# Hybrid trunk layer: decay tables computed among the projection pairs, and neighbourhood attention's first loads moved ahead of the fill's third weight block

## The chip, the cores and the metric

The kernel runs on one core of one Trainium2 chip. Its time is the device time of one execution in microseconds (us); of the kernel before there are three timed runs and one execution recorded by the profiler. Lower is better.

## What is computed

One layer of a hybrid encoder trunk on 1024 tokens of width 1024, in float32. Between two feed-forward blocks stands a token mixer, and only it is touched:

```python
u = rms_norm(x)
rq, rk, rv, rg, nq, nk, nv, g_ret, g_na = split(u @ w_in)
# retention: 4 heads, chunks of 128, forward and backward
lg    = log_sigmoid(decay_logit)                    # one number per head and direction
intra = where(lower, exp(lg * diff), 0)             # 128 x 128 per head
k_dec, q_dec = exp(lg * (127 - i)), exp(lg * (i + 1))
chunk_dec    = exp(lg * 128)
y = retention(rotary(rq), rotary(rk), rv, intra, k_dec, q_dec, chunk_dec)
y_ret = (silu(rg) * headnorm(y)) @ w_ret_out
# neighbourhood attention: 8 heads of 64, a 16 x 64 grid of tokens
y_na  = (softmax(nq nk^T / 8 + bias) nv) @ w_na_out
x = x + rms_norm((sigmoid(g_ret) * y_ret + sigmoid(g_na) * y_na) @ w_out)
```

The "decay tables" are intra for both directions, k_dec, q_dec and chunk_dec: 536 numbers in each of 128 partitions.

## The kernel before, in words

Every float32 operand of a matrix product is split into a high and a low half (`Core.split`, L62 on ScalarE makes the high half, L63 on VectorE the low one; the attention's queries use the scaled form, L65 and L66), and each product is three matmuls, high x high (L89), high x low and low x high (L90, L91). A matmul of 512 columns is the unit of PE's work.

The order of the stages around the change is this.

1. The **pairs** (`Pairs.run`, called in the loop over `jobs` in `trunk_layer`): the projections nq, nk, rq, rk, rg and the first gates, two 128-row weight tiles at a time, by Winograd's scheme with seven products, over the operands a11, s2, a12, s3, s1, a22, s4, in this order at the end of the last pair. Their results pass through `ev` tiles of the pool `pa` and are stored to DRAM by POOL's queue (L69). The weights come through `Core.raw`: a 512 KB block into one of four `wraw` buffers, loaded by SP's queue (L73), cut into two pieces of 512 columns that are split into eight `wh` and eight `wl` buffers.
2. **Neighbourhood attention** (`na_cores`): 4 pairs of heads times 8 units. The first keys (`kraw`, L891) and queries (`qraw`, four loads, L879) are loaded and split; then each unit computes scores (L921 on PE, into two PSUM banks), adds the bias while evacuating them (L922, VectorE), subtracts the maximum and exponentiates (L924, L926), divides (L928, L930), transposes the probabilities (L940, PE), splits them (`pth`, `ptl`) and multiplies them with the values (`vh`, `vl`). Its pool `na` lies in memory that the pairs used.
3. Meanwhile the **fill** gives PE work between the units: a generator, `products()`, whose steps are called by `fill(n)`. Its first products are retention's values, `vproj(wrv[j], ...)`: for three 128-token groups at a time it goes over eight 128-row slices of the weights, two slices to a W block, one step for each group and slice. `fill(n0)` issues 12 steps before the first unit, `fill(n1)` and `fill(n2)` two each in every unit. The first four slices multiply a11, the next four a12.
4. **Retention** (`ret_cores`) then reads the decay tables, which the class `Decays` computes. In the kernel before that happens at unit 12 of the attention, through the dictionary `side`; three small loads on SP (L999, L1018, L1020), some 50 small instructions on VectorE and ScalarE.

Each engine works off its own queue in order. Who stands where in it is decided when the program is built: a scheduler takes the instructions by the order of the code and by when their inputs can be there, so that loads and small instructions may be pulled far ahead of the place where the code has them. Tiles of a new pool wait for the last reader of the memory that they lie in; where a tile lies follows from the order in which the tiles are made. `add_manual_dep` with a `NoSync` dependency makes the scheduler put one instruction behind another and adds no wait.

Of the kernel before, what the change touches and what calls it, by code (L numbers as in the profile page):

```python
# [11 lines left out]
F32 = mybir.dt.float32  # L12
F32R = mybir.dt.float32r
# [6 lines left out]
P = 128  # L20
D = 1024
S = 1024
# [5 lines left out]
RH = 4  # L28
NHP = 4

NA_FILL = (12, 2, 2)
# [8 lines left out]
class Core:  # L40
# [29 lines left out]

    def raw(self, src, n=D):
        raw = self.wpool.tile([P, D], F32, tag="wraw", name="wraw", bufs=4)
        self.nc.sync.dma_start(raw[:, :n], src)  # L73
        return raw

    def piece(self, src, eng=None):

# [494 lines left out]
class LeftFactors:  # L572


    order = [j + h * FT // 2 for j in range(FT // 2) for h in range(2)]
# [289 lines left out]
    return lhs  # L865


def na_cores(c, pool, d, bias, fill, n0, n1, n2, side={}):


    nc = c.nc
    kop, qraw, qop, vop, ots, bts = {}, {}, {}, {}, {}, {}

    def qload(hp):

        qraw[hp] = [pool.tile([P, S], F32, tag="qraw", name="qraw", bufs=2) for _ in range(2)]
        for e in range(2):
            for half in range(2):
                nc.sync.dma_start(qraw[hp][e][64 * half:64 * half + 64], d["nq"][hp][64 * e:64 * e + 64])  # L879

    def qsplit(hp, cb):

# [5 lines left out]

    def load(hp):
        kr = pool.tile([P, S], F32, tag="kraw", name="kraw", bufs=1)  # L890
        nc.sync.dma_start(kr, d["nk"][hp])  # L891

        kop[hp] = [pool.tile([P, S], F32R, tag=f"k{e}", name=f"k{e}", bufs=2) for e in range(2)]
        for e in range(2):
            es, es_ = slice(64 * e, 64 * e + 64), slice(64 - 64 * e, 128 - 64 * e)
            for b in range(2):
                bs = slice(b * 512, b * 512 + 512)
                c.split(kop[hp][e][es, bs], kop[hp][e][es_, bs], kr[es, bs], eng=nc.gpsimd if hp and b else None)
# [60 lines left out]
    units = [(hp, *u) for hp in range(NHP) for u in NA_UNITS]  # L959
    n = len(units)  # L960
    s, pt = {}, {}
    load(0)
    qload(0)
    qsplit(0, 0)
    fill(n0)
    for i in range(n + 2):
        if i < n:
            s[i] = scores(*units[i])
            hp, j = units[i][0], i % 8
            if j == 4 and hp + 1 < NHP:  # L970
                load(hp + 1)
            if j in (0, 1, 4):
                qsplit(hp, {0: 1, 1: 2, 4: 3}[j])
            if j == 5 and hp + 1 < NHP:
                qload(hp + 1)
            if j == 7 and hp + 1 < NHP:
                qsplit(hp + 1, 0)
        if i in side:
            side[i]()
        fill(n1)  # L980
        if 1 <= i <= n:
            hp, _, _, cb = units[i - 1]
            if (hp, cb) not in vop:
                vload(hp, cb)
            pt[i - 1] = flip(s.pop(i - 1))
        if i >= 2:
            hp, _, rg, cb = units[i - 2]
            values(hp, rg, cb, pt.pop(i - 2))
            if (i - 2) % 8 == 7:
                c.store(d["no"][hp], ots[hp].rearrange("p r c -> p (r c)"))  # L990
        fill(n2)


class Decays:
    def __init__(self, c, pool, logits, tabs):
        nc = c.nc
        t = pool.tile([P, 8, 6], F32, name="dect")
        x = pool.tile([P, 8], F32, name="decx")
        nc.sync.dma_start(x, logits)  # L999
        a, e, z, w, s, lg = (t[:, :, i] for i in range(6))  # L1000

        nc.vector.tensor_scalar(a, x, -1.0, None, ALU.mult)
        nc.vector.tensor_tensor(a, a, x, ALU.min)
        nc.scalar.activation(e, a, AF.Exp)
# [11 lines left out]
        self.lg = lg  # L1016
# [4 lines left out]
        self.qd = pool.tile([P, 2, RH], F32, name="decq")  # L1021
        self.kd = pool.tile([P, 2, RH], F32, name="deck")
        self.gc = pool.tile([P, 2, RH], F32, name="decg")
        self.dm = pool.tile([P, RH, P], F32, name="decm")
        for b in range(2):
            ls = lg[:, 4 * b:4 * b + 4]
            nc.vector.tensor_scalar(self.qd[:, b], ls, tb[:, b:b + 1], None, ALU.mult)
            nc.vector.tensor_scalar(self.kd[:, b], ls, tb[:, 2 + b:3 + b], None, ALU.mult)
            nc.vector.tensor_scalar(self.gc[:, b], ls, 128.0, None, ALU.mult)
        for h in range(RH):  # L1030
            nc.vector.tensor_scalar(self.dm[:, h], df[:, 0], lg[:, h:h + 1], None, ALU.mult)
            nc.vector.scalar_tensor_tensor(self.dm[:, h], df[:, 1], lg[:, 4 + h:5 + h], self.dm[:, h],
                                           op0=ALU.mult, op1=ALU.add)
        for q in (self.qd, self.kd, self.gc, self.dm):
            nc.scalar.activation(q, q, AF.Exp)
        for q in (self.kd, self.dm):
            nc.vector.tensor_scalar(q, q, RET_SCALE, None, ALU.mult)
# [172 lines left out]
def trunk_layer(ctx: ExitStack, tc, x, xt, g1a, w1i, w1o, g1b, gma, wmt, wnv, wrv, logits, dtab, rope, bias,  # L1210
                wro, wno, wmo, gmb, g2a, w2i, w2o, g2b, out):
    nc = tc.nc
# [5 lines left out]
    c = Core(tc, const, wpool, psum, dram)  # L1218
    c.small = const
    pad = edge.tile([P, 32], F32, name="edge")  # L1220

    def dt(name, shape):
        return dram.tile(shape, F32, name=name)
# [8 lines left out]
        "sr": dt("sr", [8, P, S]), "sn": dt("sn", [8, P, S]), "z": dt("z", [8, P, S]), "m": dt("m", [8, 2, P, S]),  # L1232
    }

    def rows(a):
# [51 lines left out]
    def xh(t, k):  # L1287

        return a21 if (t, k) == (1, 0) else wx.op(("a11", "a12", None, "a22")[2 * t + k])

    def vproj(src, groups, done):

        for toks in groups:
            banks = {t: c.bank() for t in toks}
            for k in range(KT):
                if k % 2 == 0:
                    w = ahead.pop(k // 2) if k // 2 in ahead else c.load_w(src[k // 2])
                for t in toks:
                    tt = slice((t % 4) * P, (t % 4 + 1) * P)
                    c.mm3(banks[t], [q[:, k % 4, tt] for q in xh(t // 4, k // 4)], w[k % 2], k == 0, k == KT - 1)  # L1300
                    yield
            for t in toks:
                done(t, banks[t])
# [40 lines left out]
    with tc.tile_pool(name="pa", bufs=1, reuse_waits="tile") as pa:  # L1344
# [7 lines left out]
        tabs = [[pa.tile([P, 512], F32, tag="tab", name="tab", bufs=4) for _ in range(2)] for _ in range(2)]  # L1352
# [4 lines left out]
        for i, (_, _, f, g, fn) in enumerate(jobs):  # L1357
# [18 lines left out]
            if i == 2:  # L1376
                x1pool = pool(x1_stack, "x1b", "right")
                a21[:] = [x1pool.tile([P, 4, 512], F32R, name=f"a21{q}") for q in "hl"]
                for k in range(2):
                    raw = c.raw(d["a21"][:, 2 * k:2 * k + 2].rearrange("p k t -> p (k t)"))  # L1380
                    c.split(*[q[:, 2 * k:2 * k + 2].rearrange("p k t -> p (k t)") for q in a21], raw)
            if i == NHP - 1:
                for _ in vproj(wnv, ((4, 5, 6, 7),), done_nv):
                    pass
                for cb in range(4):
                    nc.sync.dma_start(d["nvg"][cb].rearrange("t (r c) d -> (t r) c d", r=4),
                                      d["nv"][:, KEY_OFF[cb]:KEY_OFF[cb] + 32, :])
# [1 line left out]

    m_stack, o_stack = ExitStack(), ExitStack()  # L1390
    mix = pool(m_stack, "mix")
    mix.tile([P, 40], F32, name="pad")
    evpool[:] = [mix]

    def gate(i, dst, halves=(0, 1)):
# [44 lines left out]
            c.store(d["z"][i], e)  # L1440

    fill = Filler(products())
    dec = []
    with tc.tile_pool(name="na", bufs=1, reuse_waits="tile") as na:
        na_cores(c, na, d, bias, fill, *NA_FILL, {12: lambda: dec.append(Decays(c, mix, logits, dtab))})
    dec = dec[0]
    fill.until("rv")
    with tc.tile_pool(name="ret", bufs=1, reuse_waits="tile") as ret:
        ret_cores(c, ret, mix, d, dec, fill, RET_FILL)
# [176 lines left out]
```

## Time and profile before

| | |
|---|---|
| timed runs (3) | 2257.23, 2260.53, 2262.26 us; median 2260.53 |
| profiled execution | 2262.09 us, of which the profile's span is 2260.2 us |
| PE (TensorE matmul) busy | 2200.6 us, 97% |
| DVE (VectorE) busy | 1638.3 us, 72% |
| ACT (ScalarE) busy | 984.0 us, 44% |
| POOL (GpSimd) busy | 581.0 us, 26% |
| mean granted clock of TensorE | 0.992 |

The profile is that of one execution. Its times are microseconds from the start of the span. A timeline row has start, length, engine, line, operation, what it writes and reads, shape and count, and in brackets how long the engine sat idle before it and what ended that. SPq and POOLq are the engines' DMA queues: a row there is the issue of a transfer, not its landing. PEld is TensorE's weight load. The granted clock is the share of full speed that TensorE was given.

The stretch that matters lies near 1000 us: the last pair's last product (s4) ends at 1004, the fill's first matmuls (ps<-wh,a11h) follow, and the first score matmul (L921) starts at 1018.22.

### The profile page before, as it was taken

Reading aid. Unit: us, or ns where it says so; the run is one execution under the profiler, and the core shown is the slowest. Engines: PE = TensorE matmul, PEld = TensorE weight load, DVE = VectorE, ACT = ScalarE, POOL = GpSimd, SP = SyncE. Lnnn points to the kernel's source line nnn. Section 1 sums busy time; section 2 is a strip of 40 time slices with the busy share of each in tenths; the row PEclk is TensorE's granted clock in tenths of the full one; section 3 lists DMA queues with packets and bytes.
Section 4 is the critical chain, followed back from the end, with each engine's and each line's share of the span. In section 5 each row is a group of like instructions: output and inputs, shape, how many; then the busy total and the mean of one; then the engine's idle time right before and its main releaser. Section 6 shows DMA issues by size and latency. Waiting matters only on the chain.

```text
span 2260.2 us, 30006 instructions
## 1 busy us (share of the span) xinstructions
PE 2200.6 (97%) x10200; PEld 1827.2 (81%) x10200; DVE 1638.3 (72%) x2911; ACT 984.0 (44%) x2039; POOL 581.0 (26%) x755
## 2 busy tenths in 40 slices
PE   7899999999998999999999999999999999999998
PEld 5688888888786887878888888888887888888886
DVE  7898878765458757769885678553899887876444
ACT  5444434332334322248885665422544343433232
POOL 1121212158521122311101222111112121215942
PEclk9999999999999999999999999999999999999999
DMA  6354434497545455557655466686445443449864
GB/s 251 131 183 153 177 131 174 176 388 295 201 173 181 168 173 144 146 170 246 218 184 173 151 219 228 250 307 228 145 144 213 146 171 137 154 161 363 297 223 180
DMA packets 155240, 449.34 MB, mean 199 GB/s; under 512 B 19600, under 2 KB 50448, under 8 KB 152976
## 3 DMA queue, kind: packets, MB, share of 16 engines
q1 hardware_dynamic: 112656, 311.09, 39.9%
q0 software_dynamic: 42432, 136.35, 16.6%
q8 instruction: 81, 1.33, 0.2%
q14 instruction: 71, 0.58, 0.1%
HBM read 302.66 MB, written 148.90 MB: 200 GB/s over the span
## 4 chain that ended last, share of the span: by engine, by line
PE 84%; DVE 6%; issue 3%; ACT 3%; DMA 2%; POOL 2%; SPq 0%; POOLq 0%; DVEq 0%; ACTq 0%
PE ps L91 26%; PE ps L90 26%; PE ps L89 26%; PE pt L90 1%; PE pt L91 1%; PE pt L89 1%; POOL rstd L99 1%; DVE wl L63 1%; PE ps L921 1%; PE pt L940 1%; DMA wraw<-in_dram 1%; PE pt L128 0%; POOL ry L69 0%; ACT wh L62 0%; DVE s L922 0%
## 5 line engine op out<-in xcount | busy, mean ns | idle before, releaser
L63 DVE TENSOR_TENSOR wl<-wraw,wh 128x512 fp32r<-128x512 f32 x472 | 316.9, 688 | 63.1 <-ACT wh L62 62.7
L62 ACT CAST wh<-wraw 128x512 fp32r<-128x512 f32 x476 | 274.6, 618 | 175.1 <-PE ps L90 64.3
L89 PE MATMUL ps<-wh,g 128*128 128x512 f32 x548 | 214.1, 391 | 0.4 <-DVE tmp L226 0.4
L90 PE MATMUL ps<-wl,g 128*128 128x512 f32 x548 | 213.5, 390 | 0.0
L91 PE MATMUL ps<-wh,g 128*128 128x512 f32 x548 | 213.3, 389 | 0.0
L562 ACT ACTIVATE c<-c 128x512 f32<-128x512 f32 x88 | 55.4, 632 | 198.0 <-DVE c L527 103.9
L63 DVE TENSOR_TENSOR wl<-w,wh 128x512 fp32r<-128x512 f32 x77 | 76.0, 1005 | 88.3 <-ACT wh L62 88.1
L63 DVE TENSOR_TENSOR wl<-x,wh 128x512 fp32r<-128x512 f32 x77 | 79.2, 1044 | 76.2 <-ACT wh L62 74.8
L89 PEld LDWEIGHTS ps<-wh,g 128*128 128x128 f32 x548 | 102.9, 188 | 21.8 <-DVE tmp L226 0.7
L90 PEld LDWEIGHTS ps<-wl,g 128*128 128x128 f32 x548 | 102.9, 188 | 21.4 <-DVE wl L63 0.5
L91 PEld LDWEIGHTS ps<-wh,g 128*128 128x128 f32 x548 | 102.9, 188 | 21.2
L89 PE MATMUL ps<-a11h,wh 128*128 128x512 f32 x276 | 111.5, 404 | 8.4 <-ACT wh L62 8.4
L62 ACT CAST wh<-t 128x512 fp32r<-128x512 f32 x58 | 36.0, 621 | 190.0 <-DVE t L521 189.9
L91 PE MATMUL ps<-a11h,wl 128*128 128x512 f32 x276 | 109.8, 398 | 6.3 <-DVE wl L63 6.1
L90 PE MATMUL ps<-a11l,wh 128*128 128x512 f32 x276 | 109.7, 398 | 0.1
L91 PE MATMUL ps<-a22h,wl 128*128 128x512 f32 x280 | 109.2, 390 | 0.6 <-DVE wl L63 0.6
L89 PE MATMUL ps<-a22h,wh 128*128 128x512 f32 x280 | 109.7, 392 | 0.0
L89 PE MATMUL ps<-a12h,wh 128*128 128x512 f32 x276 | 108.9, 395 | 0.5 <-ACT ev L1312 0.3
L90 PE MATMUL ps<-a22l,wh 128*128 128x512 f32 x280 | 109.1, 390 | 0.0
L91 PE MATMUL ps<-a12h,wl 128*128 128x512 f32 x276 | 107.7, 390 | 0.0
L90 PE MATMUL ps<-a12l,wh 128*128 128x512 f32 x276 | 107.5, 390 | 0.0
L89 PE MATMUL ps<-s2h,wh 128*128 128x512 f32 x232 | 92.1, 397 | 7.0 <-ACT wh L62 7.0
(430 smaller groups left out, 6290.0 us busy)
## 6 DMA issues: line engine op xcount, KB each, us to landing
wraw<-in_dram SPq DMA_DIRECT2D x204, 512.0 KB, 4.4
g<-g0s SPq DMA_DIRECT2D x44, 512.0 KB, 4.1
g<-g1s SPq DMA_DIRECT2D x44, 512.0 KB, 4.9
g<-g0a SPq DMA_DIRECT2D x33, 512.0 KB, 3.3
g<-g1a SPq DMA_DIRECT2D x33, 512.0 KB, 4.3
g0s<-gth POOLq DMA_DIRECT2D x44, 256.0 KB, 4.7
g0s<-cmb POOLq DMA_DIRECT2D x44, 256.0 KB, 3.7
g1s<-gth POOLq DMA_DIRECT2D x44, 256.0 KB, 4.5
```

The costliest lines, as they stand in the source:

```text
L62: self.done = [nc.scalar.copy(h, src).ins, (eng or nc.vector).tensor_tensor(l, src, hf, ALU.subtract).ins]
L63: (eng or nc.vector).tensor_tensor(l, src, hf, ALU.subtract).ins]
L89: mm(ps, a[0], b[0], start=start, stop=False)
L90: mm(ps, a[0], b[1], start=False, stop=False)
L91: mm(ps, a[1], b[0], start=False, stop=stop)
L99: self.nc.gpsimd.tensor_tensor(r[:, :n], ms, self.mhalf[:, :n], ALU.pow)
L562: nc.scalar.activation(gate[j], gate[j], AF.Silu)
L921: nc.tensor.matmul(bv, q[:, rg * P:(rg + 1) * P], k, start=n == 0, stop=n == 1)
L940: nc.tensor.transpose(pt[:, j * P:(j + 1) * P], s[:, i % 2, (i // 2) * P:(i // 2 + 1) * P], c.ident)
```

## The change

It has two parts.

**The decay tables** are computed in the loop over the jobs of the pairs, after job 3 in the code, into one tile `dec` of the pool `pa`, and stored to a DRAM tensor of the same shape. `Decays.make` is the old computation; the object now only gives views into a 536-wide tile. After `na_cores` the tile is loaded into the pool `mix`, and retention reads it there. With this the `side` dictionary goes, and the tables' tiles and scratch leave `mix`; a pad tile there grows from 40 to 104 columns, which shifts where the later tiles of that side lie.

**The first loads of the attention**: queries are now loaded ahead of the keys; the first output tile `ots[0]` is made between the two key tiles, which moves the second one in memory; and the names of the first loads are collected in `qk`. When the fill loads the W block of its fifth slice (`k > 3`, its third block), `Core.after` puts that load behind them.

```diff
     def raw(self, src, n=D):
         raw = self.wpool.tile([P, D], F32, tag="wraw", name="wraw", bufs=4)
-        self.nc.sync.dma_start(raw[:, :n], src)
+        self.fetch = self.nc.sync.dma_start(raw[:, :n], src).ins
         return raw
+
+    def after(self, e, names):
+        for n in names:
+            self.tc.add_manual_dep(e, n, mybir.DependencyInfo(
+                mybir.DependencyClass.NoSync, mybir.DependencyReason.DATA), reason="order")
...
-        nc.sync.dma_start(kr, d["nk"][hp])
-
-        kop[hp] = [pool.tile([P, S], F32R, tag=f"k{e}", name=f"k{e}", bufs=2) for e in range(2)]
+        first.append(nc.sync.dma_start(kr, d["nk"][hp]).ins.name)
+
+        kop[hp] = []
+        for e in range(2):
+            kop[hp].append(pool.tile([P, S], F32R, tag=f"k{e}", name=f"k{e}", bufs=2))
+            if e == 0 and not ots:
+                ots[0] = pool.tile([P, 16, 64], F32, tag="ot", name="ot", bufs=2)
...
+    qload(0)
     load(0)
-    qload(0)
     qsplit(0, 0)
     fill(n0)
...
-        if i in side:
-            side[i]()
...
 class Decays:
-    def __init__(self, c, pool, logits, tabs):
+    def __init__(self, t):
+        self.qd, self.kd, self.gc = (t[:, 8 * i:8 * i + 8].rearrange("p (b h) -> p b h", b=2) for i in range(3))
+        self.dm = t[:, 24:].rearrange("p (h t) -> p h t", h=RH)
+
+    def make(self, c, pool, logits, tabs):
...
                 if k % 2 == 0:
                     w = ahead.pop(k // 2) if k // 2 in ahead else c.load_w(src[k // 2])
+                    if k > 3 and qk:
+                        c.after(c.fetch, qk)
+                        qk.clear()
...
             if i == NHP - 1:
+                dec = pa.tile([P, 536], F32, name="dec")
+                Decays(dec).make(c, pa, logits, dtab)
+                c.store(d["dec"], dec)
...
-    mix.tile([P, 40], F32, name="pad")
+    mix.tile([P, 104], F32, name="pad")
...
-        na_cores(c, na, d, bias, fill, *NA_FILL, {12: lambda: dec.append(Decays(c, mix, logits, dtab))})
-    dec = dec[0]
+        na_cores(c, na, d, bias, fill, *NA_FILL, qk)
+    tabs = mix.tile([P, 536], F32, name="dec")
+    nc.sync.dma_start(tabs, d["dec"])
+    dec = Decays(tabs)
```

What the scheduler makes of it is seen in the built programs' queues. First SP's queue from the last weight blocks of the pairs to the attention's first value load, before. Here `in_dram` is an input of the kernel, `nvg` the gathered values, `nk` and `nq` the keys and queries in DRAM, `bt` a bias tile; lines are those of the kernel before.

```order
L1386 DMA nvg<-nv 16x16384 x4
L73 DMA wraw<-in_dram 128x1024 x21
L999 DMA decx<-in_dram 128x8
L1018 DMA dectb<-in_dram 128x4
L1020 DMA decd<-in_dram 128x256
L73 DMA wraw<-in_dram 128x1024
L1145 DMA rg<-rg 128x2x128 x2
L891 DMA kraw<-nk 128x1024
L879 DMA qraw<-nq 64x1024 x4
L911 DMA bt<-in_dram 128x768 x2
L904 DMA vraw<-nvg 128x4x128
```

The same place in the changed program (its lines run 5 to 16 higher; `dec<-dec` is the load of the tables):

```order
L1402 DMA nvg<-nv 16x16384 x4
L73 DMA wraw<-in_dram 128x1024 x16
L1462 DMA dec<-dec 128x536
L1153 DMA rg<-rg 128x2x128 x2
L885 DMA qraw<-nq 64x1024 x4
L898 DMA kraw<-nk 128x1024
L922 DMA bt<-in_dram 128x768
L73 DMA wraw<-in_dram 128x1024
L922 DMA bt<-in_dram 128x768
L915 DMA vraw<-nvg 128x4x128
L73 DMA wraw<-in_dram 128x1024 x2
```

Of the W blocks in these rows the first 14 belong to the pairs. Before, eight blocks of the fill stand ahead of the keys; now two do, the third stands behind one bias tile, and the small loads for the tables are gone to the pairs.

Next PE's queue where the first scores stand. Before, up to the second score matmul:

```order
L89 MATMUL ps<-wh,a12h 128x512
L90 MATMUL ps<-wl,a12h 128x512
L921 MATMUL ps<-k_8346,qh 128x384
L91 MATMUL ps<-wh,a12l 128x512
L89 MATMUL ps<-wh,a12h 128x512
L90 MATMUL ps<-wl,a12h 128x512
L91 MATMUL ps<-wh,a12l 128x512
L921 MATMUL ps<-k_8346,ql 128x384
```

And in the changed program:

```order
L96 MATMUL ps<-wh,a11l 128x512
L932 MATMUL ps<-k_8409,qh 128x384
L932 MATMUL ps<-k_8409,ql 128x384
L932 MATMUL ps<-k_8411,qh 128x384
L932 MATMUL ps<-k_8411,ql 128x384
L94 MATMUL ps<-wh,a12h 128x512 x2
L95 MATMUL ps<-wl,a12h 128x512
L96 MATMUL ps<-wh,a12l 128x512
```

The first unit's four score matmuls now stand together, directly behind the fill's 36 matmuls on a11; before, the first of them stood 14 fill matmuls later, and the others among further ones.

Last DVE's queue from the first key splits on. Before (`dect` is the scratch of the tables):

```order
L63 TENSOR_TENSOR k_8346<-kraw,k_8346 64x512 x2
L63 TENSOR_TENSOR k_8347<-kraw,k_8347 64x512 x2
L63 TENSOR_TENSOR wl<-wraw,wh 128x512 x2
L66 SCALAR_TENSOR_TENSOR ql<-qraw,qh 128x256 x2
L1012 TENSOR_SCALAR dect<-dect 128x8
L1011 TENSOR_TENSOR dect<-dect 128x8
```

In the changed program (L933 is the evacuation of the scores, its `nast` row reads the maximum, L935 negates it):

```order
L66 SCALAR_TENSOR_TENSOR ql<-qraw,qh 128x256 x4
L63 TENSOR_TENSOR k_8409<-kraw,k_8409 64x512 x2
L63 TENSOR_TENSOR k_8411<-kraw,k_8411 64x512 x2
L933 ISA s,nast<-ps,bt 128x384
L933 ISA nast 128x1
L63 TENSOR_TENSOR wl<-wraw,wh 128x512
L933 ISA s,nast<-ps,bt 128x384
L933 ISA nast 128x1
L63 TENSOR_TENSOR wl<-wraw,wh 128x512
L935 TENSOR_SCALAR nast<-nast 128x2
L63 TENSOR_TENSOR vl<-vraw,vh 128x512
```

The tables' instructions are gone from here, and the third W block's low halves (`wl`) stand between the first score evacuations.

More of the change, by code (lines that the diff above doesn't have):

```diff
@@ L865, in stream, with na_cores @@
     return lhs
-def na_cores(c, pool, d, bias, fill, n0, n1, n2, side={}):
+def na_cores(c, pool, d, bias, fill, n0, n1, n2, first=None):
     nc = c.nc
     kop, qraw, qop, vop, ots, bts = {}, {}, {}, {}, {}, {}
+    first = [] if first is None else first
     def qload(hp):
@@ L878, in qload @@
             for half in range(2):
-                nc.sync.dma_start(qraw[hp][e][64 * half:64 * half + 64], d["nq"][hp][64 * e:64 * e + 64])
+                e_ = nc.sync.dma_start(qraw[hp][e][64 * half:64 * half + 64], d["nq"][hp][64 * e:64 * e + 64])
+                first.append(e_.ins.name)
     def qsplit(hp, cb):
@@ L1015, in __init__ @@
         nc.vector.scalar_tensor_tensor(lg, s, -2.0, lg, op0=ALU.mult, op1=ALU.add)
-        self.lg = lg
         tb = pool.tile([P, 4], F32, name="dectb")
@@ L1020, in __init__ @@
         nc.sync.dma_start(df.rearrange("p a b -> p (a b)"), tabs[:, :256])
[L1021 to L1024, printed above, removed]
         for b in range(2):
@@ L1231, in trunk_layer @@
         "rv": dt("rv", [TT, P, D]), "rg": dt("rg", [8, P, S]), "ry": dt("ry", [8, P, S]),
-        "sr": dt("sr", [8, P, S]), "sn": dt("sn", [8, P, S]), "z": dt("z", [8, P, S]), "m": dt("m", [8, 2, P, S]),
+        "dec": dt("dec", [P, 536]), "sr": dt("sr", [8, P, S]), "sn": dt("sn", [8, P, S]), "z": dt("z", [8, P, S]), "m": dt("m", [8, 2, P, S]),
     }
@@ L1289, in xh @@
         return a21 if (t, k) == (1, 0) else wx.op(("a11", "a12", None, "a22")[2 * t + k])
+    qk = []
     def vproj(src, groups, done):
@@ L1442, in trunk_layer @@
     fill = Filler(products())
-    dec = []
     with tc.tile_pool(name="na", bufs=1, reuse_waits="tile") as na:
-        na_cores(c, na, d, bias, fill, *NA_FILL, {12: lambda: dec.append(Decays(c, mix, logits, dtab))})
-    dec = dec[0]
+        na_cores(c, na, d, bias, fill, *NA_FILL, qk)
+    tabs = mix.tile([P, 536], F32, name="dec")
+    nc.sync.dma_start(tabs, d["dec"])
+    dec = Decays(tabs)
     fill.until("rv")
```

## The prediction

> **What bounds the kernel now.** I read the page first, then the busy time by windows around the start of neighbourhood attention, then the timelines of PE and SP there, then the chain of waits.
>
> ```profile
> span 2260.2 us, 30006 instructions
> PE 2200.6 (97%) x10200; PEld 1827.2 (81%) x10200; DVE 1638.3 (72%) x2911; ACT 984.0 (44%) x2039; POOL 581.0 (26%) x755
> ```
>
> PE is the bound: 97% of the span, so a microsecond is won only where PE stands idle or runs at a lowered clock. Of the windows after 1015 us (stretch, length, then busy time of PE, PEld, DVE, ACT and POOL, granted clock, DMA share, GB/s) these matter:
>
> ```profile
> 1015.00:1020.00 5.00, 2.18 (x9) 1.49 (x8) 4.83 (x11) 3.74 (x9) 0.00 (x0) 0.96 1.04 303
> 1020.00:1025.00 5.00, 5.00 (x18) 4.13 (x18) 4.13 (x20) 2.51 (x9) 0.00 (x0) 0.70 0.15 56
> 1025.00:1030.00 5.00, 3.80 (x20) 2.71 (x19) 4.77 (x19) 5.00 (x15) 1.07 (x2) 1.00 0.82 297
> 1030.00:1060.00 30.00, 29.11 (x174) 25.13 (x174) 29.12 (x81) 26.73 (x72) 4.90 (x5) 1.00 0.77 249
> 1060.00:1200.00 140.00, 138.95 (x815) 122.61 (x814) 112.83 (x321) 112.83 (x293) 13.68 (x21) 1.00 0.64 203
> ```
>
> In the first, PE works 2.18 of 5 us; in the second it is busy throughout at 0.70 of full clock. Later attention runs almost without a gap (138.95 of 140). PE's timeline names the places:
>
> ```profile
> 1011.83 0.39 PE L91 MATMUL ps<-wh,a11l 128*128 128x512 f32 x1
> 1012.06 0.39 PE L89 MATMUL ps<-wh,a12h 128*128 128x512 f32 x1
> ...
> 1015.00 0.39 PE L90 MATMUL ps<-wl,a12h 128*128 128x512 f32 x1
> 1018.22 0.44 PE L921 MATMUL ps<-k,qh 128*128 128x384 f32 x1 [2.82 <-ACT qh L65]
> ...
> 1026.92 0.39 PE L91 MATMUL ps<-wh,a12l 128*128 128x512 f32 x1
> 1027.87 1.09 PE L940 MATMUL pt<-ident,s 128*128 128x128 f32 x6 [0.56 <-DVE s L930]
> 1029.61 0.39 PE L89 MATMUL ps<-pth,vh 128*128 128x256 f32 x1 [0.64 <-ACT pth L62]
> ```
>
> The fill's matmuls follow each other every 0.23 us (1011.83, 1012.06). The first score matmul, L921, stops this row at 1015.00: PE is an in-order queue, and the scores lack their split queries until 1018.22. Why they are late stands in SP's queue:
>
> ```profile
> 967.34 1.14 SPq L73 DMA_DIRECT2D wraw<-in_dram  x2
> ...
> 1005.42 0.33 SPq L73 DMA_DIRECT2D wraw<-in_dram  x1
> 1005.84 0.90 SPq L1145 DMA_DIRECT2D rg<-rg  x2
> 1006.91 0.41 SPq L891 DMA_DIRECT2D kraw<-nk  x1
> 1007.42 2.44 SPq L879 DMA_DIRECT2D qraw<-nq  x4
> ```
>
> The fill's first two W blocks go out at 967.34. Six more, the last at 1005.42 once its buffer is free, stand ahead of the keys' load, which then takes 7.46 us by the chain of waits:
>
> ```profile
> 1006.91 7.46 DMA kraw<-nk
> ```
>
> **What the change takes away.** The stall: 3.22 us from start to start less one pitch of 0.23 is 2.99. After it the clock is lowered: (1 - 0.96) x 5 + (1 - 0.70) x 5 = 1.70 us of lost PE time. The Trainium skill (TensorE: Matmul & The Clock Gate, section HAM oscillation — how this bites in real kernels) has it that gaps under about 3.4 us do not lower the clock; by that rule this 1.70 would not belong to the stall and the gain below would be 3.3. The trace disagrees: a 2.99 us gap is followed within 2 us by the lowered clock, and I keep the term. Before the first transposes PE loses 1027.87 - 1026.92 - 0.23 = 0.72, before the first values 0.64. Together 2.99 + 1.70 + 0.72 + 0.64 = 6.05 us between 1015 and 1030.
>
> **When the operands are ready after.** In the changed queue of SP the queries and keys stand directly behind the second W block and the two rg loads, ahead of the third W block. What they wait for is the memory that they reuse, last read by the s3 and s4 products of the last pair:
>
> ```profile
> 995.28 0.39 PE L90 MATMUL ps<-s3l,wh 128*128 128x512 f32 x1
> ...
> 1003.67 0.39 PE L91 MATMUL ps<-s4h,wl 128*128 128x512 f32 x1
> ```
>
> By the built program's waits queries and keys need s3 alone, the bias tile needs s4. So the queries go out at 995.7, four issues of 2.44 in all, the keys end at 998.6. Landing and splits:
>
> ```profile
> DMA to landing us min/median/max: 3.2/4.7/9.3
> ```
> ```profile
> 1004.82 0.63 ACT L1373 ACTIVATE ev<-ev 128x512 f32<-128x512 f32 x1 [0.27 <-DVE ev L545]
> ...
> 1014.39 2.30 ACT L62 CAST k<-kraw 64x512 fp32r<-64x512 f32 x4 [3.50 <-DMA kraw<-nk]
> ...
> 1017.75 0.72 ACT L65 ACTIVATE qh<-qraw 128x256 fp32r<-128x256 f32 x2
> ```
> ```profile
> 1015.04 2.61 DVE L63 TENSOR_TENSOR k<-kraw,k 64x512 fp32r<-64x512 f32 x4 [2.15 <-ACT k L62]
> 1017.68 1.29 DVE L63 TENSOR_TENSOR wl<-wraw,wh 128x512 fp32r<-128x512 f32 x2
> ...
> 1023.97 0.56 DVE L922 CUSTOM_DVE_ANT_0 s<-ps,bt 128x384 f32<-128x384 f32 x1 [0.80 <-PE ps L921]
> 1024.46 0.08 DVE L922 DVE_READ_ACCUMULATOR2_ANT nast<- 128x1 f32 x1
> ```
>
> The first line is qraw's landing. ACT reaches the splits behind the last pair's sigmoid, at 1005.45, by when both loads have usually landed; with the longest landing the last query comes at 998.2 + 9.3 = 1007.5. Four query casts are 2 x 0.72, four key casts 2.30, and DVE ends 0.96 after ACT (1017.65 against 1016.69): 1010.2, at worst 1012.2. PE now has the scores after the 36 a11 matmuls, at 1012.06. The stall is gone, with 1.9 us to spare, none in the worst case.
>
> **What is late next.** Two things, both new. First, the fill's fifth 128-row slice comes from the third W block. Its low half (wl) stands on DVE behind the first score evacuation. The first pair of scores ends at about 1012.4, DVE follows 0.2 later with 0.56 + 0.08, then wl takes 0.65: 1013.9. PE is there after four scores (0.7) and two matmuls, at 1013.2: 0.7 us of wait, and behind it in PE's queue stands everything else. Second, the transposes wait for the softmax. On DVE that is two evacuations and two wl to 1015.2, then ACT's Exp pair:
>
> ```profile
> 1026.81 1.39 ACT s L926 x5
> ```
>
> The pair of Exp ends near 1016.8, but DVE has the second unit's evacuations in between, whose scores PE finishes at 1013.9 + 10 x 0.23 + 0.7 = 1016.9; with 0.2 + 0.64, a reciprocal, one query split (0.4) and the scaling (0.4) the transposes can start near 1018.9. PE comes there after six more fill matmuls, one score and one matmul, at 1018.6: 0.3 us. Neither wait is near the 2.99 us that lowered the clock. New waits 1.0 us (from 0, if the evacuations come sooner, to 2.5), net 6.05 - 1.0 = 5.05.
>
> **The decay tables.** They leave this place and go among the pairs:
>
> ```profile
> 1000.00:1200.00 200.00, 7.28 (x40) 0.22 (x1) 0.99 0.67 214
> ```
> ```profile
> 728.00:765.00 37.00, 37.00 (x165) 30.66 (x164) 26.64 (x42) 10.15 (x17) 4.31 (x8) 1.00 0.50 171
> 750.00:760.00 10.00, 10.00 (x46) 8.29 (x45) 9.78 (x16) 4.17 (x8) 2.17 (x4) 1.00 0.54 193
> ```
>
> The first row is dect's alone: 40 DVE instructions of 7.28 us, most of them before or beside the stall. They now stand where DVE has 37 - 26.64 = 10.4 us idle and PE none, so I cost them at 0; without that cover they cost up to 7.28. Two table loads more on ACT,
>
> ```profile
> 1006.82 1.28 ACT L1004 ACT_TABLE_LOAD   x1
> ```
>
> 2.6 us in all, have ACT's 27 idle us in that stretch and its later pairs. The exponential's table load now stands between the first values' split and the first Exp; ACT waits there for DVE until 1015.2, which hides 1.28 if the values have landed by 1013. The store on POOL (26% busy) and the load behind SP's W blocks carry 268 KB each, and nothing reads the tables before the retention: 0. The larger pad only shifts places.
>
> **Sum.** 5.0 us less. Against the profiled execution (2262.09, span 2260.2) that is 2257.1; this one was 1.6 above the median of the three runs, so from 2260.5 I forecast 2255.5.
>
> **Rivals.** (a) The third W block is late. It is issued behind a bias tile that waits for s4, so at about 1004.6; it must land by 1012.1, to be cast before PE is through with the first scores.
>
> ```profile
> DMA to landing us min/median/max: 2.0/4.4/10.5
> ```
>
> The median of wraw, 4.4, speaks against (1009.0), kraw's 7.46 is just in time, the longest is not: 1015.1, split by 1016.5 instead of 1013.9, 2.6 us more, and with the clock lowered again 1.7: a gain of 0.7, 2259.8. It decides from a landing of 7.5 us on. The Trainium skill (DMA: Bandwidth & Descriptors, section Queues, rings and completion order) says that one queue's descriptors are taken in ring order on each DMA engine; by that the block would come early and this rival would hardly exist. The keys' 7.46 us, with 0.8 MB issued just ahead, speaks rather for sharing with later loads. Chance 0.18.
>
> (b) DVE gives it back. With fewer W blocks ahead of the keys, DVE has, counted in the two orders, split six 512-column pieces fewer when it comes to the first transposed probabilities. Six pieces of 0.65 us, 3.9 us, go behind that point, into 1030 to 1060, where DVE works 29.12 of 30 us. If DVE is the limit there, PE loses up to 3.9: 2259.4. Against it: the last decay instructions leave the same stretch, and from 1060 DVE has 27 us to spare. Chance 0.15.
>
> (c) Slower: the pairs have no room. If the decay instructions fall into stretches like 750 to 760 (DVE 9.78 of 10), weight splits and evacuations come late and PE waits: 7.28 and, past a gap like the one above, 1.7 of clock, less the gain: +4.0, 2264.5; with gaps in two places a little more. It decides once DVE lags by more than the pieces it has split ahead of PE. Chance 0.07.
>
> **How the numbers follow.** Forecast 0.60, (a) 0.18, (b) 0.15, (c) 0.07. The range: removing every wait and the clock loss from 1015 to 1200 gives 6.05 + 0.89 + 1.05 = 8.0, so 2252.5, and half a microsecond for the spread of medians; at the top it takes in (a) and (b): 2252.0 to 2260.2. About 0.2% (4.5 us) is what a measurement of this kernel can tell from no change; the forecast lies just beyond it. Faster by more: 0.53, nearly all from the forecast. Within: 0.42, from (a), (b), the forecast's weaker half and part of (c). Slower: 0.05.
>
> **What would show it.** In the changed profile: kraw and qraw issued near 996 to 999; no wait of several microseconds before the first score; granted clock 1.00 from 1015 to 1025; a short PE wait for wl after the first scores; PE without new gaps from 728 to 800. It is wrong if the scores still wait, if PE waits over 2 us for wh or wl of the third block, or if the pairs show a new PE wait.

## The result and the profile after

| | before | changed |
|---|---|---|
| median of 9 runs | 2260.53 us (2256.41 to 2262.61) | 2254.28 us (2252.43 to 2257.48) |
| ratio, 95% interval | | 0.9972 (0.9964 to 0.9980) |
| profiled execution, span | 2262.09, 2260.2 us | 2254.28, 2252.5 us |

The kernel is 6.25 us faster, by the interval 4.5 to 8.1 us; the forecast was 5.0. The page of the changed kernel: PE does the same 10200 matmuls in a shorter span.

```profile
span 2252.5 us, 29976 instructions
...
PE 2196.9 (98%) x10200; PEld 1824.7 (81%) x10200; DVE 1637.6 (73%) x2911; ACT 985.0 (44%) x2041; POOL 581.7 (26%) x756
```

SP's queue of the changed kernel, with queries and keys ahead of the third W block:

```profile
989.83 0.90 SPq L1153 DMA_DIRECT2D rg<-rg  x2
994.66 2.41 SPq L885 DMA_DIRECT2D qraw<-nq  x4
997.17 0.53 SPq L898 DMA_DIRECT2D kraw<-nk  x1
1003.01 0.35 SPq L922 DMA_DIRECT2D bt<-in_dram  x1
1003.46 0.40 SPq L73 DMA_DIRECT2D wraw<-in_dram  x1
```

ACT and DVE then split what has landed, at once behind the last pair:

```profile
1004.28 1.32 ACT L65 ACTIVATE qh<-qraw 128x256 fp32r<-128x256 f32 x4
1005.51 2.29 ACT L62 CAST k<-kraw 64x512 fp32r<-64x512 f32 x4
1008.38 1.14 ACT L62 CAST wh<-wraw 128x512 fp32r<-128x512 f32 x2 [0.58 <-DMA wraw<-in_dram]
...
1013.94 1.28 ACT L937 ACT_TABLE_LOAD   x1 [2.49 <-DVE nast L935]
```
```profile
1006.18 2.61 DVE L63 TENSOR_TENSOR k<-kraw,k 64x512 fp32r<-64x512 f32 x4
```

The last key is ready at 1008.79. PE begins the fill at 1002.82, and 36 matmuls later takes the first score with no wait:

```profile
1002.82 0.39 PE L94 MATMUL ps<-wh,a11h 128*128 128x512 f32 x1
...
1010.98 0.34 PE L932 MATMUL ps<-k,qh 128*128 128x384 f32 x1
1012.76 0.50 PE L95 MATMUL ps<-wl,a12h 128*128 128x512 f32 x1 [0.45 <-DVE wl L63]
...
1018.06 0.27 PE L951 MATMUL pt<-ident,s 128*128 128x128 f32 x1
```

The windows of the changed kernel, to be read against those of the prediction: no window has a lowered clock, PE is idle 0.57 us from 1010 to 1030 where it was idle 4.0 from 1015 to 1030, and the stretches behind do not pay for it.

```profile
1010.00:1015.00 5.00, 4.55 (x22) 3.54 (x21) 2.92 (x8) 1.68 (x2) 0.00 (x0) 1.00 0.69 253
1015.00:1020.00 5.00, 4.88 (x26) 3.98 (x25) 4.24 (x15) 4.99 (x15) 0.00 (x0) 1.00 0.88 302
1020.00:1025.00 5.00, 5.00 (x31) 4.42 (x30) 4.88 (x15) 5.00 (x13) 1.84 (x2) 1.00 0.32 130
1025.00:1030.00 5.00, 5.00 (x32) 4.47 (x31) 4.87 (x12) 4.89 (x15) 2.38 (x3) 1.00 0.62 175
1030.00:1060.00 30.00, 29.66 (x176) 25.97 (x175) 28.23 (x78) 26.09 (x71) 2.89 (x4) 1.00 0.86 266
1060.00:1200.00 140.00, 138.80 (x802) 121.16 (x802) 110.08 (x311) 112.17 (x290) 12.79 (x19) 1.00 0.65 213
```

One measure serves all that follows: the **attention stretch**, from the start of the fill's first matmul (1002.82 here) to the end of the attention's last value matmul:

```profile
1185.70 0.28 PE L96 MATMUL ps<-pth,vl 128*128 128x256 f32 x1
```

That is 1185.98 - 1002.82 = 183.16 us; before it is 188.46, from 1003.90. "Idle" is its length less PE's busy time, "clock" is the sum of (1 - granted clock) times length over 40 equal windows. What is left is the same work in each kernel; it scatters from 180.3 to 182.2 us, so a difference of 2 us between two single stretches says little. The experiments' medians and ratios stand against runs of the kernel before on the same chip, whose medians were 2260.58 to 2260.89.

| profile | median us | fill starts | stretch | idle | clock | left |
|---|---|---|---|---|---|---|
| before | 2260.53 | 1003.90 | 188.46 | 5.97 | 1.75 | 180.7 |
| before, second execution | | 1000.87 | 188.11 | 6.96 | 0 | 181.2 |
| changed | 2254.28 | 1002.82 | 183.16 | 2.11 | 0 | 181.1 |
| changed, second execution | | 1004.95 | 184.98 | 3.02 | 0 | 182.0 |
| decays only | 2259.76 | 1000.70 | 186.67 | 4.35 | 1.68 | 180.6 |
| loads only | 2265.78 | 1002.75 | 194.93 | 9.23 | 5.12 | 180.6 |
| loads, decays late | 2257.83 | 1005.90 | 184.60 | 3.31 | 0 | 181.3 |
| no order | 2259.02 | 1004.99 | 187.04 | 5.03 | 1.68 | 180.3 |
| keys first | 2261.79 | 1002.12 | 186.58 | 4.66 | 0 | 181.9 |
| keys first, second execution | | 1002.75 | 187.15 | 4.92 | 0 | 182.2 |
| no placing | 2255.20 | 1003.18 | 183.45 | 2.53 | 0 | 180.9 |
| decays three times | 2255.87 | 1003.22 | 184.70 | 3.20 | 0 | 181.5 |
| rotary on GpSimd | 2264.04 | 1016.79 | 184.21 | 2.21 | 0 | 182.0 |

The span's difference of the first two profiles, 7.7 us, is 1.08 ahead of the stretch, 5.30 in it and 1.36 behind it. The parts outside are no larger than the scatter: between two executions of one kernel the fill's start alone moves by 3.0 us (before) and 2.1 (changed).

### The profile page after: what moved, and what is told of

It reads as the page before. It is cut to its first block, busy times and chain, and to the rows that moved or that the text cites. A ratio compares the mean times of both kernels' runs of the same rounds, so it can differ in the third digit from the quotient of the medians.

```text
span 2252.5 us, 29976 instructions
## 1 busy us (share of the span) xinstructions
PE 2196.9 (98%) x10200; PEld 1824.7 (81%) x10200; DVE 1637.6 (73%) x2911; ACT 985.0 (44%) x2041; POOL 581.7 (26%) x756
## 4 chain that ended last, share of the span: by engine, by line
PE 82%; DVE 6%; ACT 4%; issue 4%; DMA 2%; POOL 2%; POOLq 0%; SPq 0%; DVEq 0%; ACTq 0%
PE ps L96 26%; PE ps L95 25%; PE ps L94 25%; PE pt L95 1%; PE pt L96 1%; PE pt L94 1%; POOL rstd L104 1%; ACT wh L62 1%; DMA wraw<-in_dram 1%; ACT s L937 1%; DVE wl L63 1%; DMA qraw<-nq 1%; DVE s L933 0%; PE pt L133 0%; ACT pth L62 0%
```

## The experiments

**Each half alone.** The theory (A) was that the gain is operands in time, brought by the order of the loads; the rival (D), that it is the 7.3 us of DVE work that leaves the attention. First the decay half: the changed kernel with the old loads.

```diff
-    qload(0)
     load(0)
+    qload(0)
...
-                    if k > 3 and qk:
-                        c.after(c.fetch, qk)
-                        qk.clear()
...
-            if e == 0 and not ots:
-                ots[0] = pool.tile([P, 16, 64], F32, tag="ot", name="ot", bufs=2)
```

> Theory A: the gain is that the first scores' operands are ready when PE comes to them, and it comes from the order of the loads. Rival D: it comes from taking 7.3 us of small VectorE instructions and two table loads out of the attention's start. This kernel has the decay tables among the pairs, and the old order of the loads (eight W blocks ahead of the keys, keys ahead of the queries, no placing of the output tile). A: the first score still stands 14 fill matmuls behind the 36 on a11, its operands are still issued near 1006 us, and the stall there is still 2 to 3.5 us: 0 to 1.5 us less than the kernel before, about 2259.5. D: most of the gain is here, 2254 to 2256, and the stall is under 1 us. Either way the pairs from 728 to 800 show no new PE wait.

Measured: 2259.76 us, ratio to before 0.9997 (0.9988 to 1.0005). SP's issues, PE's waits, and the windows behind the second wait:

```profile
998.28 1.01 SPq L1151 DMA_DIRECT2D rg<-rg  x2
...
1002.66 0.47 SPq L898 DMA_DIRECT2D kraw<-nk  x1
```
```profile
1012.79 0.45 PE L930 MATMUL ps<-k,qh 128*128 128x384 f32 x1 [0.60 <-ACT qh L65]
...
1022.40 1.12 PE L949 MATMUL pt<-ident,s 128*128 128x128 f32 x6 [1.71 <-DVE s L939]
```
```profile
1020.00:1025.00 5.00, 2.98 (x13) 1.92 (x13) 3.00 (x10) 4.99 (x15) 0.08 (x1) 0.83 0.90 271
1025.00:1030.00 5.00, 5.00 (x31) 4.65 (x30) 3.66 (x14) 3.82 (x11) 2.28 (x3) 0.82 0.85 289
```

Neither theory had this. The time is A's, but the stall is under the 1 us that D had set. It shrinks to 0.60 us, and not by D's VectorE work: the two rg loads, which stood between the last W block and the keys (prediction), go out before it, so the keys are issued 1.96 us behind the fill's first matmul instead of 3.01, and they land 6.30 us after that instead of 7.46. Most of the gain is not kept: PE then comes earlier to the first transposes and waits 1.71 us for the softmax, and the clock is lowered there. A wait removed in an in-order queue uncovers the next one.

Then the load half, with the tables computed in the attention's code as before:

```diff
+    dec = []
+    def decays():
+        dec.append(Decays(mix.tile([P, 536], F32, name="dec")))
+        dec[0].make(c, mix, logits, dtab)
...
-        na_cores(c, na, d, bias, fill, *NA_FILL, qk)
-    tabs = mix.tile([P, 536], F32, name="dec")
-    nc.sync.dma_start(tabs, d["dec"])
-    dec = Decays(tabs)
+        na_cores(c, na, d, bias, fill, *NA_FILL, qk, {12: decays})
+    dec = dec[0]
```

> The other half: the new order of the loads, with the placing, and the decay tables computed in the attention's code as before. In this program their small loads wait for the s2 product of the last pair (about 988 us) and their VectorE instructions stand ahead of the query splits. A: they run between 992 and 1003 beside the last pair, the operands are ready within 1 us of PE's coming, and nearly the whole gain is here: 2254 to 2257. If they run later, up to 7.3 us of VectorE work lies between the landing and the splits, and a stall of 2 to 5 us comes back. D: no gain, 2259 to 2261.

Measured: 2265.78 us, ratio 1.0023 (1.0014 to 1.0033): **slower** than before by 5.2 us, and 11.5 above the changed kernel; A's 2254 to 2257 and D's 2259 to 2261 both miss it, and the stall is longer than the 2 to 5 us that A allowed for. DVE's timeline shows why. The tables' first input had been issued at 989, but DVE comes to it behind the last pair's evacuation; then its serial chain runs until 1014.9, and the key splits stand behind it:

```profile
1002.95 0.69 DVE L550 TENSOR_TENSOR ev<-ps,ev 128x512 f32<-128x512 f32 x1 [2.03 <-PE ps L96]
1003.58 0.16 DVE L1017 TENSOR_SCALAR dect<-decx 128x8 f32<-128x8 f32 x1
...
1005.87 0.18 DVE L1020 TENSOR_SCALAR dect<-dect 128x8 f32<-128x8 f32 x1 [1.93 <-ACT dect L1019]
...
1014.50 0.43 DVE L1047 TENSOR_SCALAR dec<-dec 128x512 f32<-128x512 f32 x1 [0.61 <-ACT dec L1045]
1014.84 0.75 DVE L66 SCALAR_TENSOR_TENSOR ql<-qraw,qh 128x256 fp32r<-128x256 f32 x2
1015.63 2.61 DVE L63 TENSOR_TENSOR k<-kraw,k 64x512 fp32r<-64x512 f32 x4
```
```profile
1016.97 0.69 PE L932 MATMUL ps<-k,qh 128*128 128x384 f32 x1 [5.89 <-DVE k L63]
```

That chain takes 11 us of DVE's queue for 7.3 of work: the dependent links start 0.21 us apart though each is busy for 0.18, two of them wait for ACT (1.93 and 0.61 us), and one pair of query splits (0.75 us) stands in between.

```profile
1015.00:1020.00 5.00, 2.72 (x7) 2.02 (x8) 4.91 (x12) 3.90 (x8) 0.00 (x0) 0.50 0.00 0
1020.00:1025.00 5.00, 5.00 (x21) 4.13 (x20) 4.06 (x13) 3.82 (x10) 0.00 (x0) 0.83 0.58 181
```

PE stands for 5.89 us, and the windows behind show the clock at 0.50, then 0.83. So neither half gives the gain; the new order of the loads gives it only if the tables do not stand ahead of the splits in DVE's queue.

Is it the place of these 7.3 us, or that they are in the attention at all? The same kernel, with the tables' first load put behind the second head pair's loads:

```diff
-        nc.sync.dma_start(x, logits)
+        c.after(nc.sync.dma_start(x, logits).ins, qk)
```

> The new order of the loads, with the decay tables in the attention's code as before, but their first load put behind the second head pair's keys and queries. In this program no decay instruction stands ahead of the first query and key splits on VectorE; the first comes some 40 rows later, the rest among the later units. Theory A': where these 7.3 us stand in VectorE's queue matters, not that they are in the attention: the first scores wait under 0.5 us and the time is that of the changed kernel plus what the busy stretch from 1030 on gives back, 0 to 3 us: 2253.5 to 2257.5. Rival: the attention has no room for them (VectorE is busy 28 of 30 us from 1030 to 1060), 5 to 7 us are lost wherever they stand: 2259 to 2261.5.

Measured: 2257.83 us, ratio 0.9987 (0.9977 to 0.9996), 8 us better than the last kernel by the place alone. The first scores don't wait. What remains against the changed kernel is a wait of the transposes for the softmax's DVE steps, here in the list of PE's waits in the attention, which the changed kernel's first profile does not have:

```profile
PE pt L951 <- DVE s L941: 2.4, 3, 1.6
```

The place accounts for most of it. The rest, what the pairs' free time is worth, is 3.5 us by the medians and at most 1.4 by the stretch. Part of the distance between these two is the clock: the timed runs were granted 0.9943 of it in the mean, the changed kernel's 0.9950, which over the span is some 1.6 us. Where in the execution it was lost is not on record for timed runs.

**The order of the loads.** The changed kernel without the dependency on the third W block (the `if k > 3 and qk` lines go):

> The changed kernel without the dependency that puts the third W block behind the first loads. In this program the queries and keys stand behind six more W blocks again, and PE has 34 fill matmuls on a12 between the a11 ones and the first score, which then follow each other for three units without fill between. A: the operands are in time at 1019 us all the same (keys issued near 1006, split by 1016.5), but the fill of the first group is used up: the first transposes wait 3 to 5 us for the softmax with nothing to cover it. Gain 0 to 3: 2257.5 to 2260.5. Rival (the placing and queries ahead of keys are what matters, the dependency is not): within 1.5 us of the changed kernel, 2253 to 2256.

Measured: 2259.02 us, ratio 0.9992 (0.9983 to 1.0000). As A had it: the fill's matmuls are spent ahead of the scores, and the softmax stands bare.

```profile
1027.58 1.09 PE L951 MATMUL pt<-ident,s 128*128 128x128 f32 x6 [3.73 <-DVE s L941]
```

With the keys ahead of the queries (`load(0)` above `qload(0)`), everything else as changed:

> The changed kernel with the keys' load ahead of the queries' again; the decay tables, the placing and the third W block as changed. In this program the scheduler then puts the first three units' twelve score matmuls directly behind the a11 ones, with three fill matmuls between them and the first transposes. Theory A (the gain is operands in time, and it holds only while fill matmuls cover the softmax): the first scores wait under 0.5 us, but the twelve scores wait for VectorE's evacuations (six of 0.64 us against 2.1 us of matmuls, 1.5 to 2 us) and the transposes for the softmax (1 to 2.5 us), with or without a lowered clock: 2256.5 to 2260. Rival (the order of these two loads doesn't matter, all land in time): within 1.5 us of the changed kernel, 2253 to 2256.

> The kernel with the keys ahead of the queries once more: its profiled execution took 186.6 us for the attention, 3.4 more than the changed kernel, but its median is 7.5 us above the changed kernel's. If its waits are near the length at which the clock is sometimes lowered (1.5 and 1.2 us in the first profile), this execution has one or two of them lowered by 1.7 us each: 188 to 190 us. Else the attention takes 186 to 187 us again, and the rest of the median is open.

Measured: 2261.79 us, ratio 1.0006 (0.9997 to 1.0015). PE's waits in the stretch, first execution:

```profile
PE ps L94 <- ACT wh L62: 1.5, 1, 1.5
PE pt L951 <- DVE s L941: 1.2, 1, 1.2
PE pt L951 <- DVE ptl L63: 0.8, 1, 0.8
PE ps L932 <- DVE nast L933: 0.7, 1, 0.7
```

Two swapped lines made the scheduler set twelve scores in a row, and the order of the fill lost its use as cover. The transposes' wait at the start did not come; the third W block's cast did (1.5 us). The second execution gave 187.15 us with no lowered clock in the stretch, the second of the two cases expected, and so a loss of some 2.8 us there (two executions of each, 186.9 against 184.1). The median lies above the expected 2256.5 to 2260 and 7.5 above the changed kernel's. The clock has a part in that: 0.9936 in the mean of the timed runs against 0.9950, or some 3 us over the span. Which waits lowered it is open.

Without the placing of the first output tile (the `ots[0]` lines go):

> The changed kernel without the placing of the first output tile between the two key tiles. In this program the first casts of the keys then wait for the s3 and s4 products of the last pair as well. These end by 1003 us, the casts begin at 1005.5 behind the sigmoids. A: no difference from the changed kernel beyond 1.5 us, 2253 to 2256. Rival: the waits are on the path, and the operands come 1 to 3 us later, past the 2.2 us that they had to spare: 2256 to 2258.

Measured: 2255.20 us, ratio 0.9979 (0.9970 to 0.9987), stretch 183.45. No difference that the intervals show, as A had it: the placing takes waits away that had long ended.

**Room among the pairs.** The tables computed three times into the same tile:

```diff
-                Decays(dec).make(c, pa, logits, dtab)
+                for _ in range(3):
+                    Decays(dec).make(c, pa, logits, dtab)
```

> The changed kernel with the decay tables computed three times over among the pairs, into the same tile: 14.6 us more of VectorE, four more table loads on ScalarE. Theory A: the pairs have room (VectorE idles a quarter of their time and its weight splits run ahead of PE), so nothing or under 1.5 us: 2253 to 2256. Rival (c) of the prediction: late splits and evacuations, up to 14.6 us and a lowered clock: 2258 to 2270, with a new PE wait for wl or wh between 720 and 880.

Measured: 2255.87 us, ratio 0.9979 (0.9970 to 0.9988), as the changed kernel within the intervals. The window where the copies fall, changed and then threefold: DVE goes from 34.59 to 48.10 of 50 us, PE loses 0.01.

```profile
750.00:800.00 50.00, 50.00 (x222) 41.14 (x221) 34.59 (x60) 15.25 (x26) 6.50 (x12) 1.00 0.46 161
```
```profile
750.00:800.00 50.00, 49.99 (x221) 41.06 (x220) 48.10 (x146) 17.50 (x37) 6.59 (x12) 1.00 0.52 174
```

**A second execution** of each of the two kernels.

> The kernel before once more, for a second look at its stall and clock. Theory A: the first score waits 2.5 to 3.2 us for the queries again, the first transposes 0.5 to 0.8, the first values 0.5 to 0.8. Of the clock: in the profiles so far the clock after a gap of 1.7 to 3.4 us on PE either stayed at 1.00 or lost 1.70 us in one piece, in the same place of the program differently from one execution to the next; so after this stall it is lowered by 1.70 us with a chance of about 0.7, or not at all.

> The changed kernel once more, for a second look. From the first fill matmul to the attention's last value product it took 183.2 us in the first profile, of which PE idled 2.1 and lost nothing to the clock; the kernel before took 188.5 and 188.1. Theory A: 183 to 184.7 again (184.7 was the longest with the same order of the first scores). If it is over 186, the difference between the two kernels in this stretch was chance.

Measured: the kernel before waits again, and this time its clock stays at 1.00 there; a later wait for `pth` is longer instead (1.60 us):

```profile
1014.99 0.44 PE L921 MATMUL ps<-k,qh 128*128 128x384 f32 x1 [2.62 <-ACT qh L65]
1023.52 1.09 PE L940 MATMUL pt<-ident,s 128*128 128x128 f32 x6 [0.77 <-DVE s L930]
...
1036.47 0.39 PE L89 MATMUL ps<-pth,vh 128*128 128x256 f32 x1 [1.60 <-ACT pth L62]
```

Its windows stand in the last section. The changed kernel's stretch was 184.98 us, a little over the 184.7 of the expectation and under the 186 set as the limit. The kernel before has 188.1 and 188.5 in two profiles, the changed order of the first scores 183.2 to 185.0 in five, so the difference is not chance. The whole executions say nothing like this: this one of the changed kernel took 2259.97 us, that of the kernel before 2259.23. Ahead of the stretch the changed kernel's clock was lowered seven times for 1.70 us, that of the kernel before four times, and its fill starts 4.1 us later. A single whole execution cannot tell these two kernels apart.

**The same reading elsewhere**, an attempt at a kernel faster than both. Near 868 PE waits 2.39 us for a `wl` behind rotary products on DVE; half of these go to GpSimd.

```diff
-    tt(t, x, sin, ALU.mult)
+    c.nc.gpsimd.tensor_tensor(t, x, sin, ALU.mult)
```

> The changed kernel, and beyond it: half of the rotary products of the pairs (four tiles of 128x512 in each of four jobs) go from VectorE to GpSimd. In all profiles so far PE waits 2.39 us near 868 for a low half (wl) that stands on VectorE behind six rotary products of 0.69 us. Theory A' (what stands ahead of an operand in the in-order queue sets when it comes): three of these products are out of its way, about 2.1 us, the wait falls to under 0.5 us, and 2 to 2.5 us are won against the changed kernel (with the clock, lowered there in 2 of 10 profiles, 0.3 more on the mean): 2251 to 2253. Rival: GpSimd's products are slower than VectorE's and share its memory, VectorE slows beside them or the stores come later, and the tiles come free later: no gain or a loss, 2253.5 to 2258.

Measured: 2264.04 us, ratio 1.0017 (1.0009 to 1.0026). The rival was right, and too mild:

```profile
L1051 POOL TENSOR_TENSOR ev<-ev,tab 128x512 f32<-128x512 f32 x16 | 26.2, 1639 | 22.1 <-DVE ev L532 20.8 <-DVE ev L547 1.2
```
```profile
872.74 0.69 DVE L1052 TENSOR_TENSOR ev<-ev,tab 128x512 f32<-128x512 f32 x1 [4.56 <-POOL ev L1051]
...
880.62 0.69 DVE L1052 TENSOR_TENSOR ev<-ev,tab 128x512 f32<-128x512 f32 x1 [3.67 <-POOL ev L1051]
881.22 0.69 DVE L63 TENSOR_TENSOR wl<-wraw,wh 128x512 fp32r<-128x512 f32 x1
```
```profile
881.97 0.80 PE L96 MATMUL ps<-a11h,wl 128*128 128x512 f32 x1 [9.21 <-DVE wl L63]
```

A product takes 1.64 us on GpSimd against 0.69, the second product of the same tile waits for it in DVE's queue, and the `wl` waits behind that: 9.21 us in place of 2.39. Taking work off a queue helps only if nothing left in the queue waits for it.

## Why the prediction was right, point by point

**What is taken away (6.05).** The stall and the two waits behind it were real: by idle time 2.82, 0.56 and 0.64 us in the first profile, 2.62, 0.77 and 0.45 in the second (start-to-start differences had made the first two a little large). They are gone. As idle time the sum came out: forecast 2.99 + 0.72 + 0.64 less 1.0 of new waits, 3.35; measured 4.02 less 0.57, 3.45. The 1.70 of clock was taken as sure, and that was wrong: after the same stall in the second execution it did not come. So it is partly luck that the whole sum fits; over many runs the clock's part does come near 1.70 ("The size" below). The rule of the Trainium skill that was weighed there (TensorE: Matmul & The Clock Gate, section HAM oscillation — how this bites in real kernels) does not hold for this kernel: at the four places of the last section with gaps of 1.77 to 3.4 us, a lowered clock followed in 28 of 51 cases.

**Operands ready.** Forecast 1010.2 against PE's 1012.06, 1.9 us to spare; measured 1008.79 against 1010.98, 2.2 to spare. The queue reading (queries at 995.7, keys done at 998.6; measured 994.66 and 997.70) was right to about 1 us, the amount by which this execution ran ahead.

**New waits (1.0).** The wait for `wl` was 0.45 us instead of 0.7; that for the transposes under 0.2 instead of 0.3. Right in kind, somewhat large.

**The decay tables at 0.** In the pairs they cost nothing that the runs show, even three times over. But the step that gave all the gain to the loads and left the tables' departure at nothing failed as an account of causes: "most of them before or beside the stall" was true of the old order, not of the new one. With the new loads they would have stood ahead of the query and key splits, for 11.5 us. The sum came out because the change has both halves. And the exponential's table load was not hidden as said: it stands in ACT's queue with its Exp's wait for `nast`, begins at 1013.94, and lies in the softmax chain with its 1.28 us. It cost nothing, because DVE was with the second unit's scores until 1016.76. Not every table load waits so: the one at 968.26 in the same trace starts at once, and ACT waits 4.28 us behind it; why they differ is not shown.

**The rivals.** (a), the third W block late: issued at 1003.46, cast at 1008.38, so 4.9 us at most, under the 7.5 from which it decides. (b), DVE giving it back from 1030 to 1060: PE is busy 29.66 there, before 29.11. (c), no room in the pairs: PE stays at 37.00 of 37 where the tables run, while DVE goes from 26.64 to 34.06.

```profile
728.00:765.00 37.00, 37.00 (x164) 30.41 (x163) 34.06 (x82) 12.40 (x23) 5.41 (x10) 1.00 0.52 180
```

**The size.** Five profiles have the changed kernel's order of first scores (changed twice, no placing, three times, rotary on GpSimd); their stretch is 184.1 us in the mean, that of before 188.3: 4.2 us. The median says 6.25, at least 4.5. The timed runs tell where most of the remainder lies, since each has its mean granted clock on record: 0.9950 in the mean of the changed kernel's nine, 0.9939 in that of 77 runs of the kernel before, a difference of some 2.5 us over the span. Among runs with the same granted clock (0.994, 0.995, 0.996) the changed kernel is 4.9, 4.1 and 4.1 us faster, near the 4.2 of the stretch. So some 2 us of the 6.25 are clock. How much of these the change earns by leaving fewer gaps, and how much is the chance of nine runs, is open: the kernels without the placing and with the tables three times were granted 0.9944 and 0.9947.

## What to carry to other kernels

Before an operand is moved ahead, write down what would then stand between its landing and its use on every in-order queue it passes: here the loads alone cost 5 us, the small work alone gave nothing measurable, and both gave 6. Price a stall by following the queue on to the next wait, and look at whether matmuls are left to cover it. Cost two parts of a change together and apart; their sum is not the whole.

## What the hardware showed beyond this

The clock falls in pieces of 3.41 us at 0.50, which cost 1.70 us each where PE has work. In thirteen profiles a gap on PE was followed by none, one or more of them, and the same gap at the same place of the program did both:

| gap on PE, us | near | lowered in |
|---|---|---|
| 1.55 | 617 | 0 of 13 |
| 1.18 and 0.97, 0.7 us apart | 1720 | 5 of 13 |
| 1.77 | 38 | 6 of 13 |
| 1.8 to 2.0 | 70 | 8 of 13 |
| 2.39 | 870 | 2 of 12 |
| 3.3 to 3.4 | 717 | 12 of 13, twice by two pieces |
| 3.6 to 5.1 | 690 | 13 of 13, three times by two |
| 5.1 to 5.6 | 112 | 13 of 13, always by two |

So no length of a gap decides alone. The records of the granted clock in the traces show more. Within one execution the lowered pieces start whole multiples of 3.413 us apart: in the first profile of the kernel before at 39.95, 70.67, 111.63, 688.48, 719.20, 1019.58 and 1722.72, which are 9, 12, 169, 9, 88 and 206 of them from one to the next. Laid on this grid, the stall before the first scores reads so in the two executions of the kernel before:

```profile
1016.16:1019.58 3.42, 1.36 (x6) 1.07 (x7) 3.36 (x8) 2.29 (x6) 0.00 (x0) 1.00 1.05 319
1019.58:1022.99 3.41, 3.41 (x10) 2.76 (x9) 3.27 (x17) 1.58 (x5) 0.00 (x0) 0.50 0.34 129
```
```profile
1010.21:1013.62 3.41, 2.16 (x10) 1.46 (x8) 1.78 (x3) 2.41 (x5) 0.00 (x0) 1.00 1.01 224
1013.62:1017.04 3.42, 2.05 (x9) 1.66 (x10) 3.29 (x10) 2.20 (x6) 0.00 (x0) 1.00 1.06 319
1017.04:1020.45 3.41, 3.41 (x17) 2.63 (x16) 3.38 (x17) 2.34 (x9) 0.00 (x0) 1.00 0.28 109
```

In the first, most of the gap falls into one window of the grid: PE is busy for 1.36 of 3.42 us, and the next window has half the clock. In the second the gap is cut in two, PE is busy for 2.16 and 2.05, and nothing follows. Over all thirteen profiles, from 27 us after the start to 30 us before the end, a window at full clock in which PE was busy for less than 0.45 of the time was followed by a lowered one in 52 of 52 cases, one of 0.45 to 0.55 in 14 of 37, one above 0.55 in none of 8183. This is a pattern read from the traces, with PE's busy time as they model it; no run was made to test it.

So a stall is its length and, if it leaves one of these windows less than about half busy, 1.70 on top; two short gaps in one window can do it as well as a long one. Where the grid lies against a gap differs from one execution to the next. With that, one profile can't price the clock: the 77 timed runs of the kernel before were granted 0.991 to 0.996, those at 0.996 took 2257.1 us in the mean and those at 0.993 2262.0.
